# Last gate projection in 128-channel columns, mixed with row pairs by seven of the out-projection's left half

## The chip, the core and the metric

The kernel runs on one core of a Trainium2 chip, as one program. The metric is the device time of one execution in microseconds (us), as a median of several runs. The engines are called here as in the profile: PE (TensorE, matmuls), DVE (VectorE), ACT (ScalarE), POOL (GpSimd) and SP (SyncE, which here issues most transfers).

## What is computed

A decoder trunk of two layers on one sequence of 256 positions with 2048 channels, everything in float32:

```python
# each of 2 layers; x is 256 x 2048
h  = rmsnorm(x) * g
P  = h @ W_in                 # 2048 -> [q | k | v | gate_B | gate_C | conv_in], 1024 each
A  = differential attention (8 heads, q/k norm, shared relative bias)
Cv = gate_B * causal_depthwise_conv3(gate_C * conv_in)
x  = x + concat([A, Cv]) @ W_out        # 2048 -> 2048, "out-projection"
x  = x + (relu(rmsnorm(x) @ W_up) ** 2) @ W_down      # 8192 wide
```

The changed place is the projection for gate_B (the "last gate", since it is computed last of the six) and the out-projection that follows it.

## The kernel before

**Precision.** A float32 operand is split in two float32r parts, high and low, so that a = hi + lo. A product is made of three matmuls, the list `TERMS`: hi x hi, hi x lo, lo x hi. So each weight tile that arrives ("raw") costs one ACT copy, which makes the high part (L322), and one DVE subtraction, which makes the low part (L323). High and low parts rotate through three buffers each, raw tiles through four.

**Weights.** A class `Weights` holds a list of jobs in the order in which PE will want the tiles; each job issues a load on SP's queue and the two split instructions, some tiles ahead of their use. `take()` hands the next tile to the matmuls. Work that is not on PE's line (attention, norms, biases) is written as generators, and `work.tick()` between matmuls lets them emit their next instructions. So the order of instructions on each engine is fixed when the program is built, and each engine works its list in order.

**The mixer of a layer.** q, k and v come by halves, attention runs as background work, then gate_C and conv_in by quarters of 256 channels, with the convolution after each (`cv`), and then the last gate in four quarters (`linear_t`, L433, PE tile `gb`). `joined` (L445, L448) adds the two halves of the accumulator, `gate` (L742 to L745) multiplies by `cv`, and `in_parts` (L738, L739) writes the high and low parts into `cat`, the left operand of the out-projection: `cat` 0 and 1 hold attention, 2 and 3 the gated convolution.

**The out-projection** (`BySeven.project`) runs over two halves of 1024 output columns, left (g = 0) and right (g = 1), each of two chunks of 512 columns. Its 2048 input rows are eight "row pairs" of 2 x 128. An ordinary pair takes 24 matmuls of 128x512 for both chunks (L851). A pair "by seven" is taken as a product of 2x2 blocks with seven block products in place of eight (after Winograd's form of Strassen's method): 21 matmuls (L876). For that it needs sums of blocks on both sides. Left side: `sums_of` (L780 to L786), four small additions and a split. Weights: two raw tiles are loaded (L807); `w7b` is the split left tile (L793, L794), `w7t` four sums of weight blocks (L822, L823, L826, L827), `w7x` and `w7y` their splits, and half of the right tile goes through an ordinary high and low buffer (as `whi`, `wlo`). In each half two of eight pairs go by seven, those of gate quarters 0 and 1. The seven products are put together once, after the last pair by seven (`es`, `e2`, `es4`), and added to the residual `xs`. After the left half the norm of the MLP starts on the residual's first chunks (transposes `tpn`).

**The MLP's up-projection** already runs by 128-channel columns: `up_part` (L1172) uses a weight tile of 16 x 128 x 128 in two halves, and its accumulator is one PSUM bank with the tag `av`, of which there is one buffer.

Of the kernel before, what the change touches and what calls it, by code (L numbers as in the profile page):

```python
# [15 lines left out]
P = 128  # L16
# [22 lines left out]
GATED = (0, 1)  # L39
# [83 lines left out]
def trunk(ctx: ExitStack, tc: tile.TileContext, x, w_in, w_out, conv_w, q_norm_g, k_norm_g,  # L123
# [142 lines left out]
    def load_bias(l, bpool, bias, setup):  # L266
# [11 lines left out]
        for h in range(0, NH, 2):  # L278
            for j in range(2):
                late(nc.scalar.activation(bias[:, j * NH + h:j * NH + h + 2],  # L280
                                          revs[j][:, h:h + 2, ::-1], AF.Copy))
            yield 2
# [24 lines left out]
    class Weights:  # L307
# [80 lines left out]

        def turned(self, w, col):
            for i in range(D // P // 4):  # L390
                self.plain(w, 4 * P * i, col, 4)

# [217 lines left out]
    def attention(l, qT, kT, kL, v, h0, dst, bias, tmp, pace):  # L610
# [9 lines left out]
        def unit(i):  # L620
# [19 lines left out]
            for t in range(NT):  # L640
                W = (t + 1) * P
                for m in range(2):
                    nc.vector.tensor_tensor_reduce(
                        out=s[:, m, OFF[t]:OFF[t] + W], in0=sc[t][:, m],
                        in1=bias[:, 2 * h + m, S - W:], op0=ALU.add, op1=ALU.max, scale=1.0,
                        scalar=-3.0e38, accum_out=mx[:, t, m:m + 1])
# [59 lines left out]
            yield 12 * pace  # L706
            for t in range(NT):
# [4 lines left out]
                tp3 = tp.rearrange("p (h c) -> p h c", c=P)  # L712
# [22 lines left out]
    def in_parts(dst, j, value):  # L735

        hi, lo = (dst.open()[:, i, 2 * j:2 * j + 2] for i in range(2))
        nc.scalar.activation(hi, value, AF.Copy)  # L738
        nc.vector.tensor_sub(lo, value, hi.bitcast(F32))  # L739
        dst.ready = j == 1  # L740
# [10 lines left out]
    class BySeven:  # L751
# [3 lines left out]
        def __init__(self, l, bpool, weights):  # L755
            self.l, self.pool, self.weights = l, bpool, weights
            n = D // (4 * P)
            seven = [n + q for q in GATED]
            plain = [i for i in range(2 * n) if i not in seven]


            self.orders = []
            for g in range(2):
                chunks = (2 * g, 2 * g + 1)
                order = [(n, i) for n in chunks for i in plain[:2]]
                for i, j in zip(plain[2:], seven):
                    order += [("seven", j), ("pair", i)][::-1 if g else 1]
                order += [("pair", i) for i in plain[2 + len(seven):-2]]
                order += [(n, i) for n in chunks for i in plain[-2:]]
                self.orders.append(order)  # L770
            self.sums = []

        def sums_of(self, q, y):

            if len(self.sums) % 2 == 0:
                room = self.pool.tile([P, 2, 2, 4, P], F32R, tag="b", name="sf")
                self.sums += [room[:, 0], room[:, 1]]
            a11, a21, a12, a22 = (y[:, k, t * P:(t + 1) * P] for k in range(2) for t in range(NT))
            v = wide(f"sv{q}").rearrange("p (s c) -> p s c", c=P)
# [4 lines left out]
            hi, lo = (self.sums[GATED.index(q)][:, part] for part in range(2))  # L784
# [3 lines left out]
        def jobs(self, w, i, col):  # L788
# [8 lines left out]
            def two(pool, tag, name, src):  # L797

                room = pool.tile([P, 2, 2, CH], F32R, tag=tag, name=name)
# [3 lines left out]
            def plain():  # L803
# [9 lines left out]
                b11, b21 = two(self.pool, "b", "w7b", raws[0])  # L813
# [4 lines left out]
            def sums():  # L818
                left, right = mine["raw"]
                t = mine["t"] = self.pool.tile([P, 4, CH], F32, tag="b", name="w7t")  # L820
# [3 lines left out]
                made = two(apool, "a", "w7x", t[:, 0:2])  # L824
# [5 lines left out]
            def more():  # L830
                return two(apool, "a", "w7y", mine["t"][:, 2:4])
# [3 lines left out]
        def project(self, g, cat, norm, kpool, tmp):  # L835
            weights, order = self.weights, self.orders[g]
            both = [mm.tile([P, NT, CH], F32, tag="mm2", name=f"o{self.l}{2 * g + n}")
                    for n in range(2)]
            accs = [[acc[:, t] for t in range(NT)] for acc in both]
            prods = {2: accs[0][0], 4: accs[0][1], 3: accs[1][0]}  # L840

            def plain(i, n):
                hi, lo = weights.take()
                for j in range(2):
                    k = 2 * i + j
                    a = cat[k // KG]
                    while not a.ready:
                        work.tick()
                    for t in range(NT):
                        for m, (pa, pw) in enumerate(TERMS):  # L850
                            nc.tensor.matmul(  # L851
                                accs[n][t], a.ap[:, pa, k % KG, t * P:(t + 1) * P],
                                (hi, lo)[pw][:, j], start=(k == 0 and m == 0),
                                stop=(i == last and j == 1 and m == 2))
                    work.tick()

            def form(i, pa, a):
                q = i - D // (4 * P)
                if a >= S1:
                    return self.sums[GATED.index(q)][:, pa, a - S1]  # L860
                k, t = 2 * i + a // 2, a % 2
                return cat[k // KG].ap[:, pa, k % KG, t * P:(t + 1) * P]

            def seven(i, start, end):
                if start:
                    for n in (1, 5, 6):
                        prods[n] = bank(f"po{self.l}{g}{n}")
                    prods[7] = ps.tile([P, CH], F32, tag="av", name=f"po{self.l}{g}7", bufs=1)
# [3 lines left out]
                for n, a, b in ((1, A11, b11), (2, A12, b21), (3, S4, b22), (5, S1, t1),  # L872
                                (7, S3, t3), (6, S2, t2), (4, A22, t4)):
                    own = n in (1, 5, 6, 7)
                    for m, (pa, pw) in enumerate(TERMS):
                        nc.tensor.matmul(prods[n], form(i, pa, a), b[pw],  # L876
                                         start=(start and own and m == 0),
                                         stop=(end and own and m == 2))
# [4 lines left out]
            def onto(n):  # L883
                for t in range(NT):
                    nc.vector.tensor_add(xs[2 * g + n][:, t], accs[n][t], xs[2 * g + n][:, t])

            last = order[-1][1]
            steps = [i for what, i in order if what == "seven"]
            done = [j for j, (what, i) in enumerate(order) if what == 2 * g][-1]
            for j, (what, i) in enumerate(order):  # L890
                if what == "pair":
                    plain(i, 0)
                    plain(i, 1)
                elif what == "seven":
                    seven(i, i == steps[0], i == steps[-1])
                    if i == steps[-1]:

                        x11, x21, x12, x22 = (xs[2 * g + n][:, t]
                                              for n in range(2) for t in range(NT))


                        room = tmp.tile([P, 2, CH], F32, tag="ao", name="es", bufs=1)
# [582 lines left out]
```

## Time and profile before

| what | value |
|---|---|
| median of 3 runs | 2122.43 us (2122.37 to 2122.54) |
| profiled execution | 2122.24 us |
| its span from first to last instruction | 2120.4 us |
| granted TensorE clock | 1.000 |
| PE busy | 2115.1 us |
| DVE busy | 1748.2 us |
| ACT busy | 1382.2 us |
| POOL busy | 159.2 us |
| mean DMA rate | 224 GB/s |
| last gate, layer 0 (from, length) | 253.34, 44.53 us |
| last gate, layer 1 | 1307.88, 44.53 us |

Rows of the profile read as follows. A group of instructions shows line, engine, operation, output tile <- input tiles, sizes, count, then busy time and the mean nanoseconds of one, then the idle time of the engine just before them and what ended it. In the timeline a row is start, length, engine and instruction, with the idle time before it in brackets. In the chain a row is start, length and a run of instructions of one engine. In the waits a row is the waiting instruction, the one that released it, the time in total, the number of times, and the longest.

### The profile page before, as it was taken

The numbers are of one execution on the slowest core, as the hardware profiler recorded it, in microseconds if no ns is written. First come the engines' busy times: TensorE is split into PE (matmuls) and PEld (weight loads), VectorE is DVE, ScalarE is ACT, GpSimd is POOL, SyncE is SP. The second block draws the span as 40 slices with busy tenths as digits, with TensorE's granted clock in tenths as the row PEclk, the third lists the DMA queues.
The fourth block names the chain that finished last, engine by engine and source line by source line (L and its number), as shares of the span: only waits on it lengthen the run. The fifth ranks groups of instructions, "written<-read, shape, count | busy, mean of one in ns | idle before, by whom it ended". The sixth has DMA issues, their size and how long they took to land.

```text
span 2120.4 us, 29268 instructions
## 1 busy us (share of the span) xinstructions
PE 2115.1 (100%) x10845; PEld 1807.6 (85%) x10845; DVE 1748.2 (82%) x2428; ACT 1382.2 (65%) x1838; POOL 159.2 (8%) x226
## 2 busy tenths in 40 slices
PE   9999999999999999999999999999999999999999
PEld 7888888888888888888888888888888888888887
DVE  6777678898888888799766776788988888888997
ACT  6776555676776776666566765557777677675664
POOL 3010100000000000011101101000000000000110
PEclk9999999999999999999999999999999999999999
DMA  8546666787777777788655565658877777777993
GB/s 279 175 154 205 193 194 191 251 257 226 230 233 233 230 236 230 248 299 293 213 169 182 162 212 179 199 169 267 258 229 235 231 232 233 231 229 261 319 309 104
DMA packets 297744, 476.02 MB, mean 224 GB/s; under 512 B 12707, under 2 KB 193781, under 8 KB 297600
## 3 DMA queue, kind: packets, MB, share of 16 engines
q1 hardware_dynamic: 269120, 406.76, 60.1%
q0 software_dynamic: 28288, 67.24, 9.9%
q8 instruction: 85, 1.39, 0.3%
q14 instruction: 59, 0.48, 0.1%
q10 hardware_dynamic: 192, 0.15, 0.0%
HBM read 440.52 MB, written 33.58 MB: 224 GB/s over the span
## 4 chain that ended last, share of the span: by engine, by line
PE 99%; ACT 1%; issue 0%; DVE 0%; DVEq 0%
PE upc L1172 31%; PE pr L1215 14%; PE dn L1296 8%; PE o L851 6%; PE ci L433 4%; PE gc L433 4%; PE gb L433 4%; PE k L408 4%; PE q L408 4%; PE v L408 4%; PE dn L1378 2%; PE dn L1215 2%; PE pr1r L1215 2%; PE pr0r L1215 1%; PE up L1172 1%; PE upw L1172 1%
## 5 line engine op out<-in xcount | busy, mean ns | idle before, releaser
L1172 PE MATMUL upc<-nT,uhi 128*128 128x512 f32 x1920 | 454.7, 389 | 0.0
L323 DVE TENSOR_TENSOR wlo<-raw,whi 128x1024 fp32r<-128x1024 f32 x258 | 311.8, 1222 | 156.9 <-ACT whi L322 85.6
L1172 PEld LDWEIGHTS upc<-nT,uhi 128*128 128x128 f32 x1920 | 360.3, 188 | 74.7
L322 ACT ACTIVATE whi<-raw 128x1024 fp32r<-128x1024 f32 x258 | 272.8, 1059 | 230.1 <-PE gb L433 28.0
L1036 DVE TENSOR_TENSOR ulo<-uraw,uhi 128x1024 fp32r<-128x1024 f32 x256 | 311.7, 1221 | 110.7 <-ACT f L1204 91.5
L1035 ACT ACTIVATE uhi<-uraw 128x1024 fp32r<-128x1024 f32 x256 | 270.6, 1057 | 157.8 <-PE upc L1172 137.5
L1172 PEld LDWEIGHTS upc<-nT,ulo 128*128 128x128 f32 x1920 | 246.2, 191 | 9.3
L1172 PE MATMUL upc<-nT,ulo 128*128 128x256 f32 x1920 | 249.1, 283 | 0.0
L1296 PE MATMUL dn<-whi,fb 128*128 128x512 f32 x496 | 156.5, 389 | 0.0
L851 PE MATMUL o<-whi,cat 128*128 128x512 f32 x384 | 122.0, 391 | 0.0
L1061 ACT ACTIVATE b2h<-draw 128x1024 fp32r<-128x1024 f32 x83 | 88.2, 1063 | 48.5 <-PE pr L1215 41.3
L322 ACT ACTIVATE whi<-uraw 128x1024 fp32r<-128x1024 f32 x62 | 65.9, 1062 | 81.8 <-PE dn L1296 66.0
L1296 PEld LDWEIGHTS dn<-whi,fb 128*128 128x128 f32 x496 | 93.1, 188 | 19.2
L1182 ACT ACTIVATE ev<-upc 128x512 f32<-128x512 f32 x120 | 72.0, 600 | 54.5 <-PE upc L1172 54.5
L1061 ACT ACTIVATE t24h<-t 128x1024 fp32r<-128x1024 f32 x83 | 88.3, 1063 | 22.8 <-PE pr L1215 15.9
L1062 DVE TENSOR_TENSOR t24l<-t,t24h 128x1024 fp32r<-128x1024 f32 x83 | 101.1, 1218 | 1.7
L1062 DVE TENSOR_TENSOR b2l<-draw,b2h 128x1024 fp32r<-128x1024 f32 x83 | 100.9, 1215 | 1.1 <-ACT b2h L1061 1.1
L1062 DVE TENSOR_TENSOR t13l<-t,t13h 128x1024 fp32r<-128x1024 f32 x83 | 101.0, 1217 | 0.7
L1075 DVE TENSOR_TENSOR t<-draw 128x1024 f32<-128x1024 f32 x83 | 101.1, 1218 | 0.3
L1061 ACT ACTIVATE t13h<-t 128x1024 fp32r<-128x1024 f32 x83 | 88.4, 1065 | 13.3 <-DVE t L1075 2.9
L1296 PE MATMUL dn<-wlo,fb 128*128 128x512 f32 x248 | 96.5, 389 | 0.0
L1215 PE MATMUL pr<-t13h,f 128*128 128x512 f32 x240 | 93.8, 391 | 0.0
(447 smaller groups left out, 4296.3 us busy)
## 6 DMA issues: line engine op xcount, KB each, us to landing
uraw<-in_w_up_dram SPq DMA_DIRECT2D x128, 1024.0 KB, 6.3
raw<-in_w_in_dram SPq DMA_DIRECT2D x191, 512.0 KB, 4.3
draw<-in_w_down_dram SPq DMA_DIRECT2D x174, 512.0 KB, 5.2
raw<-in_w_out_dram SPq DMA_DIRECT2D x64, 512.0 KB, 4.2
uraw<-in_w_down_dram SPq DMA_DIRECT2D x62, 512.0 KB, 5.7
raw<-in_w_down_dram SPq DMA_DIRECT2D x10, 1024.0 KB, 5.4
hid0p<-f POOLq DMA_DIRECT2D x19, 512.0 KB, 3.6
fb<-hid0p POOLq DMA_DIRECT2D x19, 512.0 KB, 7.5
```

Of the source, the lines that this page charges most:

```text
L322: pair = (nc.scalar.activation(hi, raw, AF.Copy), nc.vector.tensor_sub(lo, raw, hi.bitcast(F32)))
L323: nc.vector.tensor_sub(lo, raw, hi.bitcast(F32)))
L408: nc.tensor.matmul(acc[:, t], a.ap[:, pa, k % KG, t * P:(t + 1) * P], (hi, lo)[pw][:, j], start=(k == 0 and (pa, pw) == (0, 0)), stop=(k = ...
L433: nc.tensor.matmul(acc[:, f, 0] if part else acc[:, f], wt[:, k % 4, fs], a.ap[:, 0, k % KG] if part else a.ap[:, :, k % KG], start=(part ...
L851: nc.tensor.matmul(accs[n][t], a.ap[:, pa, k % KG, t * P:(t + 1) * P], (hi, lo)[pw][:, j], start=(k == 0 and m == 0), stop=(i == last and ...
L1035: pair = (nc.scalar.activation(hi, src, AF.Copy), nc.vector.tensor_sub(lo, src, hi.bitcast(F32)))
L1036: nc.vector.tensor_sub(lo, src, hi.bitcast(F32)))
L1061: keep(nc.scalar.activation(hi, src, AF.Copy))
L1062: keep(nc.vector.tensor_sub(lo, src, hi.bitcast(F32)))
L1172: nc.tensor.matmul(acc[:, 0] if part else acc, wt[part][:, k], a.ap[:, 0, k % KG] if part else a.ap[:, :, k % KG], start=(part == 0 and kh ...
L1215: nc.tensor.matmul(prods[n], f[:, pa, a], b[pw], start=(start and m == 0), stop=(stop and m == 2))
L1296: nc.tensor.matmul(prods[p], f[:, pa, 2 * k + t], b[pw][:, n], start=(p in starts and k == 0 and m == 0), stop=(stop and k == 1 and m == 2))
```

## The change

The last gate and the left half of the out-projection become one stage with an order written out by hand, `LEFT`. The gate comes in eight columns of 128 channels ("c"), each with two raw tiles of 8 x 128 rows by 128 columns (512 KB, rows of 512 bytes) and the `av` bank as accumulator, except for the first. Between them stand the row pairs by seven, cut in two: "a" is products 1, 2, 3 and 5 (12 matmuls), "b" is products 7, 6 and 4 (9 matmuls). Six of the eight row pairs of the left half go by seven (0 to 5): four of attention and two of the gated convolution. Pairs 6 and 7 are ordinary, and the entries (chunk, pair) place their halves. The right half keeps two pairs by seven (now 2 and 3, of attention), each after an ordinary pair.

To that end: attention's output is first evicted whole (`ay`), then split, and the sums for pairs 0 to 3 are made in attention's background work; the gate is evicted, added, multiplied and split column by column; the bias tile becomes two halves in a pool of two buffers, which later holds `w7x` and `w7y`; `w7t` of the left half takes `kL`'s place; and the results of the products by seven of the left half are added to the residual after the last matmul of that half, together with the ordinary accumulators.

The diff, cut to its core:

```diff
-GATED = (0, 1)
+LEFT = (("c", 0), ("c", 1), ("a", 0), ("c", 2), ("b", 0), ("c", 3), ("a", 1), ("c", 4), ("b", 1),
+        ("c", 5), ("a", 2), ("c", 6), ("b", 2), ("c", 7), ("a", 3), ("b", 3), (0, 6),
+        ("a", 4), ("b", 4), (1, 6), (0, 7), ("a", 5), ("b", 5), (1, 7))
+SEVEN_LEFT = tuple(i for what, i in LEFT if what == "a")
+SEVEN_RIGHT = (2, 3)
...
+        def column(self, w, col):
+            def half(kh):
+                def make():
+                    raw = self.pool.tile([P, 8, P], F32, tag="raw", name="raw", bufs=RAW)
+                    nc.sync.dma_start(
+                        raw, w[kh * 8 * P:(kh + 1) * 8 * P, col:col + P].rearrange(
+                            "(k p) c -> p k c", p=P))
+                    return self.halves(raw)
...
+    def column_part(acc, acts, weights):
+        tiles = [weights.take() for _ in range(2)]
+        for part in range(2):
+            for kh, wt in enumerate(tiles):
+                for k in range(8):
+                    a = acts[kh * 2 + k // KG]
+                    nc.tensor.matmul(
+                        acc[:, 0] if part else acc, wt[part][:, k],
+                        a.ap[:, 0, k % KG] if part else a.ap[:, :, k % KG],
...
-                hi = parts[:, 0, :, t * P:(t + 1) * P]
-                nc.scalar.activation(hi, tp3, AF.Copy, scale=s_gain[:, l:l + 1])
-                nc.vector.scalar_tensor_tensor(
-                    parts[:, 1, :, t * P:(t + 1) * P], tp3, s_gain[:, l:l + 1], hi.bitcast(F32),
-                    op0=ALU.mult, op1=ALU.subtract)
+                y = wide(f"ay{h0}_{t}")
+                nc.scalar.activation(y, tp, AF.Copy, scale=s_gain[:, l:l + 1])
+                ys.append(y.rearrange("p (h c) -> p h c", c=P))
+                hi = parts[:, 0, :, t * P:(t + 1) * P]
+                nc.scalar.activation(hi, ys[t], AF.Copy)
+                nc.vector.tensor_sub(parts[:, 1, :, t * P:(t + 1) * P], ys[t], hi.bitcast(F32))
+                yield 2
+            for j in range(2):
+                sums_of(h0 // 2 + j, *(ys[t][:, 2 * j + k] for k in range(2) for t in range(NT)))
                 yield 2
...
-    def gate(q, acc, cv, dst, y):
-        g = joined(acc, f"gb{q}")
-        nc.vector.tensor_mul(y, g, cv[:, q * 2:q * 2 + 2])
-        in_parts(dst, q % 2, y)
+    def gate(c, acc, cv, dst, y):
+        ev = nat.tile([P, 2, S], F32, tag="wide", name=f"gb{c}")
+        nc.scalar.activation(ev, acc, AF.Copy)
+        nc.vector.tensor_add(y, ev[:, 0], ev[:, 1])
+        nc.vector.tensor_mul(y, y, cv[:, c])
+        hi, lo = (dst.open()[:, i, c % KG] for i in range(2))
+        nc.scalar.activation(hi, y, AF.Copy)
+        nc.vector.tensor_sub(lo, y, hi.bitcast(F32))
...
+        def left_jobs(self, w_gate, col, w):
+            for what, i in LEFT:
+                if what == "c":
+                    weights.jobs += weights.column(w_gate, col + i * P)
+                elif what == "a":
+                    made[i] = self.jobs(w, i, 0)
+                    weights.jobs += made[i][:2]
+                elif what == "b":
+                    weights.jobs += made[i][2:]
+                else:
+                    weights.plain(w, 2 * P * i, what * CH, 2)
...
+            for j, (what, i) in enumerate(LEFT):
+                if what == "c":
+                    column(i)
+                elif what == "a":
+                    b11, b21, b22 = weights.take()
+                    self.t1, self.t3 = weights.take()
+                    self.product(1, i, A11, b11, start, end)
+                    self.product(2, i, A12, b21, start, not {"a", 0} & rest)
+                    self.product(3, i, S4, b22, start, not {"a", 1} & rest)
+                    self.product(5, i, S1, self.t1, start, end)
+                elif what == "b":
+                    t2, t4 = weights.take()
+                    self.product(7, i, S3, self.t3, start, end)
+                    self.product(6, i, S2, t2, start, end)
+                    self.product(4, i, A22, t4, start, not {"b", 0} & rest)
+                    if end:
+                        add = self.results(0)
+                else:
+                    self.pair(i, [(what, accs[what])], ...)
+                    if j == len(LEFT) - 1:
+                        add()
+                        for n in range(2):
+                            for t in range(NT):
+                                nc.vector.tensor_add(xs[n][:, t], accs[n][t], xs[n][:, t])
...
-            biasp = scope.enter_context(tc.tile_pool(name="biasp", bufs=1))
+            biasp = scope.enter_context(tc.tile_pool(name="biasp", bufs=2))
...
-            for q in range(AW // WC):
-                acc = linear_t(f"gb{l}{q}", hT, weights)
-                gate(q, acc, cv, cat[2 + q // 2], ys[:, q])
-                if q in GATED:
-                    by_seven.sums_of(q, ys[:, q])
+            by_seven.left(hT, cv)
```

More of the change, by code (lines that the diff above doesn't have):

```diff
@@ L749, in trunk, with __init__ @@
     A11, A21, A12, A22, S1, S2, S3, S4 = range(8)
     class BySeven:
-        def __init__(self, l, bpool, weights):
+        def __init__(self, l, bpool, biasp, tmp, weights):
             self.l, self.pool, self.weights = l, bpool, weights
[L757 to L779, printed above, removed]
+            self.biasp, self.tmp = biasp, tmp
+            self.pairs = range(D // (2 * P))
+            plain = [i for i in self.pairs if i not in SEVEN_RIGHT]
@@ L830, in more, with form, product, pair @@
             def more():
-                return two(apool, "a", "w7y", mine["t"][:, 2:4])
+                room = self.biasp.tile([P, 2, 2, CH], F32R, tag="bias", name="w7y")
+                return two(room, mine["t"][:, 2:4])
             return [plain, sums, more]
[L835 to L843, printed above, removed]
+        def form(self, i, pa, a):
+            if a >= S1:
+                return self.sums[i][pa][:, a - S1]
+            k, t = 2 * i + a // 2, a % 2
+            return self.cat[k // KG].ap[:, pa, k % KG, t * P:(t + 1) * P]
+        def product(self, n, i, a, b, start, stop):
+            for m, (pa, pw) in enumerate(TERMS):
+                nc.tensor.matmul(self.prods[n], self.form(i, pa, a), b[pw],
+                                 start=(start and m == 0), stop=(stop and m == 2))
+        def pair(self, i, chunks, starts=(), last=False):
+            for n, accs in chunks:
+                hi, lo = self.weights.take()
                 for j in range(2):
                     k = 2 * i + j
-                    a = cat[k // KG]
+                    a = self.cat[k // KG]
                     while not a.ready:
@@ L874, in seven @@
                     own = n in (1, 5, 6, 7)
[L875 to L878, printed above, removed]
+                    self.product(n, i, a, b, start and own, end and own)
                     if n == 5:
```

218 lines of the change are left out of this document (140 added, 78 removed).

## The prediction

> **What bounds the kernel now.** The page comes first: its busy shares and its chain.
>
> ```profile
> PE 2115.1 (100%) x10845; PEld 1807.6 (85%) x10845; DVE 1748.2 (82%) x2428; ACT 1382.2 (65%) x1838; POOL 159.2 (8%) x226
> ...
> PE 99%; ACT 1%; issue 0%; DVE 0%; DVEq 0%
> ```
>
> Then the waits of PE, which say what it ever stood still for:
>
> ```profile
> PE warm L177 <- DVE mhalf L169: 1.1, 1, 1.1
> PE q L408 <- ACT whi L348: 0.2, 1, 0.2
> ```
>
> PE multiplies from end to end and waits 1.3 us, all at the start. So a removed matmul is worth its whole spacing, and every stall that the new order makes costs its whole length. The windows of the stage that changes in layer 0 (last gate, first and second part of the out-projection) and, last, of the MLP's up-projection show how much room the feeding engines have:
>
> ```profile
> 253.30:297.90 44.60, 44.60 (x258) 39.44 (x257) 30.72 (x42) 22.84 (x27) 2.15 (x1) 1.00 0.59 189
> 297.90:347.00 49.10, 49.10 (x220) 40.63 (x220) 39.31 (x46) 25.50 (x33) 0.00 (x0) 1.00 0.62 195
> 347.00:397.00 50.00, 50.00 (x252) 42.13 (x251) 43.93 (x65) 31.05 (x48) 0.89 (x2) 1.00 0.62 206
> 408.00:480.00 72.00, 72.00 (x388) 62.46 (x387) 68.14 (x93) 51.56 (x63) 3.22 (x5) 1.00 0.78 246
> ```
>
> After the length come the busy times of PE, PEld, DVE, ACT and POOL. DVE has 14 of 44.6 us free beside the gate and 10 of 49 beside the left half. The up-projection, which already mixes 128-channel columns with products by seven, has 68.14 of 72 on DVE and still no PE wait. The granted clock is 1.00 throughout, so the clock is no part of this.
>
> **What is saved.** The chain in order of time gives the matmul spacings:
>
> ```profile
> 253.34 44.53 PE gb L433 x256
> ...
> 373.22 10.88 PE o L851 x48
> ...
> 424.33 5.54 PE upc L1172 x32
> ```
>
> A 128x512 matmul follows the last one after 10.88/48 = 0.2267 us. An ordinary row pair over both chunks takes 24 of them, by seven 21. The left half goes from two pairs by seven to six: 4 x 3 = 12 fewer in each layer, 24 in all, 24 x 0.2267 = 5.44 us. The gate keeps its 256 matmuls a layer; 32 of the old form take 44.53/8 = 5.566, 32 of the column form (the up-projection's) 5.54: 16 columns save 0.42. Saved on PE: **5.86 us**, 0.28% of the time. Nothing else on PE changes its count.
>
> **What is added off PE.** Rows for the prices:
>
> ```profile
> L323 DVE TENSOR_TENSOR wlo<-raw,whi 128x1024 fp32r<-128x1024 f32 x39 | 46.9, 1221 | 21.4 <-issue 14.6 <-ACT whi L322 5.9 <-PE gb L433 0.9
> L322 ACT ACTIVATE whi<-raw 128x1024 fp32r<-128x1024 f32 x37 | 39.2, 1060 | 36.0 <-PE gb L433 14.1 <-PE o L851 13.8 <-issue 5.4
> L794 DVE TENSOR_TENSOR w7y<-w7t,w7y 128x1024 fp32r<-128x1024 f32 x4 | 4.9, 1224 | 0.1
> L793 ACT ACTIVATE w7b<-raw 128x1024 fp32r<-128x1024 f32 x4 | 4.2, 1060 | 8.4 <-DMA raw<-in_w_out_dram 8.4
> L822 DVE TENSOR_TENSOR w7t<-raw 128x512 f32<-128x512 f32 x4 | 2.7, 686 | 0.3 <-DMA raw<-in_w_out_dram 0.3
> L786 DVE TENSOR_TENSOR sf<-sv,sf 128x512 fp32r<-128x512 f32 x2 | 1.4, 686 | 0.0
> L1183 DVE TENSOR_TENSOR h<-ev 128x256 f32<-128x256 f32 x128 | 53.1, 417 | 0.0
> L445 ACT ACTIVATE gb0l<-gb 128x512 f32<-128x512 f32 x2 | 1.2, 600 | 1.6 <-PE gb L433 1.6
> ```
>
> So DVE takes 1.22 for 1024 elements, 0.68 for 512, 0.42 for 256; ACT 1.06 for 1024 and 0.60 for an eviction. One pair by seven is three DVE subtractions of 1.22 and five of 0.68: 7.1 us, against 21 x 0.2267 = 4.76 on PE: DVE loses 2.3 on each. A column costs DVE 2 x 1.22 + 3 x 0.42 = 3.7 against 5.54. Over the left stage (174 x 0.2267 + 8 x 5.54 = 83.8 us of PE) that is 6 x 7.1 + 8 x 3.7 + four ordinary splits 4.9 + sums for two pairs 3.6 = 81 us at full durations. Consecutive instructions overlap, as ACT's timeline shows (1.06 long, the next begins 0.98 later), and by 0.08 on each of some 120 the sum falls to about 72. DVE is therefore 86 to 97% full: the average just fits. What decides is order, as DVE and ACT work their lists in order. The timeline of ACT beside the old gate:
>
> ```profile
> 260.83 1.06 ACT L322 ACTIVATE whi<-raw 128x1024 fp32r<-128x1024 f32 x1 [2.69 <-PE gb L433]
> 262.64 1.06 ACT L322 ACTIVATE whi<-raw 128x1024 fp32r<-128x1024 f32 x1 [0.75 <-PE gb L433]
> 264.51 0.60 ACT L445 ACTIVATE gb0l<-gb 128x512 f32<-128x512 f32 x1 [0.81 <-PE gb L433]
> 266.35 1.06 ACT L322 ACTIVATE whi<-raw 128x1024 fp32r<-128x1024 f32 x1 [1.24 <-PE gb L433]
> 267.33 0.63 ACT L738 ACTIVATE cat<-ys 128x512 fp32r<-128x512 f32 x1
> ```
>
> ACT stands 2.69 us at a weight split until PE leaves a buffer (three high and three low parts rotate), and whatever is listed behind stands too. Below, c0 to c7 are the columns, a0 to a5 and b0 to b5 the two parts of a pair by seven (12 and 9 matmuls).
>
> **Step 1: a2 waits for its weights, 2.7 us a layer.** In the built order ACT has, behind the eviction of c4: w7x of a2, the split of c6's first half, w7y of a2, the sums' high part, a cat part, and only then w7b of a2; DVE has w7y, c6's first half, the sums, cat, w7b. Yet PE needs w7b first, right after c5. The split of c6's first half needs the buffer that c5's first half leaves: 8 x 0.2267 = 1.81 after c5's start. From there: w7y's high part starts 0.98 later and ends at 3.85; then on DVE w7y 1.22, c6 1.22, sums 0.68, cat 0.42, w7b 1.22 = 4.76, less 4 x 0.08. End 8.3, with the handovers between engines 8.3 to 8.7. PE comes to the product with w7b's low part at 5.54 + 0.23 = 5.77. Late by 2.5 to 2.9; I take 2.7. Nothing hides it: PE has nothing else, since its own list is in order as well.
>
> **Step 2: evictions behind loads, 1.9 us a layer.** Columns c1 to c7 share one PSUM bank, so c2 starts only after the eviction of c1. That stands on ACT behind both splits of c2 and w7y of a0. The raw buffers (four) are the chain:
>
> ```profile
>   ACT w7b L793: 17.8, 8
> ...
> DMA to landing us min/median/max: 3.3/4.3/10.3
> ```
>
> ```profile
> raw<-in_w_in_dram SPq DMA_DIRECT2D x19, 512.0 KB, 3.6
> ```
>
> (first the view of the raw tile: ACT waited 17.8 us in 8 cases for a raw load; then one row of the DMA view of 230 to 400 us, the gate's loads, median 3.6). The low split of c0's second half ends at the earliest 0.3 after c0's start (its buffer leaves PE before the last low pass, 8 x (5.54 - 16 x 0.2267)/16 = 0.96 ahead of it; then 1.22). Then: load for a0 4.3, two w7t 1.29, an addition of 128x512 0.6, low split of c1's second half 1.22 (it stands on DVE behind w7t), load for c2 4.6, its high split 1.06, w7y 0.98, eviction 0.60 = 14.65; end 14.95. PE could start c2 at 2 x 5.54 + 2.72 = 13.80. Late by 1.15, with handovers some 1.4. Behind that eviction on ACT are queued c3's splits and the cat parts, so they come later by as much. With loads at the fast end of 3.3 it is nothing; with column loads a microsecond slower 2.6. The same figure returns at c4, where c3's eviction stands behind c4's splits, w7y of a1, a cat and the sums: reckoned on from the late c2, 0.5 (0 to 2.7). A load of a column's half has 512-byte rows; before has none of such size, and its rows of 1 KB and more have the median 4.3, which is why I take 4.6 here.
>
> The Trainium skill, page "DMA: Bandwidth & Descriptors", sections "Specifications" and "Why small descriptors are slow (HBM only)", says that 512 B is the least for line rate on the one hand, and that each packet costs some 3 cycles on top of its 32-byte beats on the other: 19 cycles for 512 B against 35 for 1 KB, by my estimate 9% more for the same bytes. By the first a column's load would cost what others do and c2 would come 0.3 earlier; by the second it would be 4.7. No run so far shows such a load.
>
> **Step 3: tail and seam, 0.9 us a layer.** At the stage's end ten raw tiles are wanted in some 25 us through four buffers: 10 x 4.3/4 = 11 fits, but each behind another's split: 0.4 (0 to 1.5). The results of products by seven now all come after b5: ten DVE steps of 0.60 to 0.68, behind two splits of 1.22, before the residual's first chunk is whole. From the sixth product (0.6 before b5's end) that is 8.4 to 9.2, thus 7.8 to 8.6 after b5, while PE works off (1,7) and two pairs of the right half, 36 x 0.2267 = 8.16, and then transposes that chunk: 0.5 (0 to 1.0).
>
> Edits at nothing: sums for pairs 0 to 3 inside attention, whole attention output first (a few 0.68s on DVE, whose stage has room and no PE wait); biases in two buffers; the same bytes on SP's queue, POOL's multiplications unmoved.
>
> **Sum.** 2.7 + 1.9 + 0.9 = 5.5 a layer, 11.0 for two; layer 1 has the same lists but for one exchange. 2122.24 (the profiled execution: span 2120.4 and 1.8 around it) - 5.86 + 11.0 = 2127.4; the median stands 0.2 above that execution: **2127.6 us**. Ends: only step 1, 2122.4 - 5.86 + 5.4 = 2122.0; everything at its upper end, (2.9 + 5.3 + 2.5) x 2 = 21.4, 2138. A measurement of this kernel tells about 0.2%, 4.2 us, from no change: faster is below 2118.2, slower above 2126.7.
>
> **Rivals.**
> Faster: no stall, as in the up-projection, which has the same interleaving at 95% of DVE and no PE wait. What speaks against it: there one load feeds two columns, so half as many loads stand ahead of evictions, and step 1's order is not found there. 2122.4 - 5.86 = 2116.6; it decides if w7b's low part is done by 5.8 us after c5's start. Up to 1.6 us of stalls would still be faster (2118.2). 0.15.
> No change that can be told: step 1, and of the others 0 to 2 us a layer: 2122 to 2126; half of step 1 alone would give 2119.3. Speaks for it that the gate's loads land in 3.6. 0.33.
> Slower, as forecast or worse: 0.52. The worse half is slow 512-byte rows: each column load a microsecond longer lengthens steps 2 and 3 by about 2 us a layer: 2131.5, and up to 2138. Speaks for it the maximum of 10.3; against it the low DMA share of 0.6.
> That fewer matmuls are saved is excluded by the built order: 174 for 186 in each layer.
>
> **The numbers.** The range from 2118 leaves out nearly all of the faster rival (0.14), up to 2136 some 0.06. The forecast's own range is 2126.7 to 2136.
>
> **What would show it.** PE's waits, 1.3 us now, should hold a2's product on DVE's w7b with two times 2.5 to 2.9; columns c2 and c4 on ACT's eviction; the transposes on DVE's residual add. PE's busy time should fall by 5.9. Wrong am I if the waits stay under 6 us in sum, most of all if w7b shows none; then DVE's or ACT's order was not the limit. If column loads take over 5.5, the time goes to the upper end.

## Result and the profile after

The changed kernel takes **2141.44 us** (median of 4 runs, 2139.46 to 2142.54) against 2122.40 before (4 runs, 2122.29 to 2122.54): ratio 1.0088, 95% interval 1.0074 to 1.0103, 19.0 us slower. The forecast was 2127.6 with a range up to 2136. The sign was right, the size was not: the loss against the saving of 5.86 us is 24.9, and 11.0 had been forecast.

Busy time and chain on the page of the changed kernel:

```profile
PE 2119.0 (99%) x10821; PEld 1805.0 (84%) x10821; DVE 1794.7 (84%) x2540; ACT 1405.0 (66%) x1886; POOL 171.3 (8%) x226
...
PE 89%; DVE 5%; DMA 4%; issue 1%; ACT 1%; SPq 0%; DVEq 0%; ACTq 0%
```

The count of matmuls fell by 24, as forecast (10845 to 10821), but PE's busy time rose by 3.9 us where it should have fallen by 5.9: on average a matmul stands longer. And a tenth of the chain, which was nearly all PE, now lies elsewhere (the chain follows a late result back through work that ran beside PE, so this share is not idle time). The waits of PE:

```profile
PE po L887 <- DVE w7b L833: 4.4, 2, 2.2
PE gb L417 <- ACT gb L774: 3.6, 4, 1.3
PE po L887 <- ACT w7b L832: 2.7, 2, 1.8
PE po L901 <- DVE wlo L327: 2.2, 3, 1.1
PE tpn L511 <- DVE x L1005: 1.7, 2, 1.2
...
PE po L887 <- DVE w7y L833: 0.9, 1, 0.9
PE o L901 <- DVE wlo L327: 0.8, 2, 0.5
```

Sixteen waits, 16.3 us (before: 1.3, at the start, and those are still there). Three of these rows are the three steps of the prediction by name: w7b for a2, the evictions of columns (`gb`) for c2 and c4, and the residual (`x`) for the transposes. Now the same stage by windows (start:end, length, PE, PEld, DVE, ACT, POOL busy, granted clock, DMA share, GB/s); the second and the last row are the stretch in which a2 is late, in layer 0 and in layer 1:

```profile
253.60:299.20 45.60, 43.65 (x235) 37.16 (x234) 38.90 (x63) 25.79 (x35) 7.09 (x1) 1.00 0.64 189
299.20:307.60 8.40, 4.44 (x14) 3.36 (x14) 6.73 (x9) 3.56 (x6) 0.00 (x0) 0.80 0.55 166
307.60:354.96 47.36, 44.59 (x208) 36.31 (x207) 37.12 (x48) 23.61 (x29) 0.00 (x0) 1.00 0.49 162
1319.00:1365.00 46.00, 44.34 (x242) 37.94 (x240) 40.40 (x63) 26.73 (x38) 7.10 (x1) 1.00 0.64 192
1365.00:1375.50 10.50, 7.33 (x19) 5.54 (x19) 7.51 (x11) 4.82 (x7) 0.00 (x0) 0.67 0.50 155
```

Elsewhere in these stages the granted clock is 1.00. In single microseconds of that stretch it is 0.50:

```profile
304.00:305.00 1.00, 1.00 (x3) 0.81 (x3) 1.00 (x2) 0.00 (x0) 0.00 (x0) 0.50 0.85 262
```

And PE's own timeline there, in layer 0:

```profile
297.13 2.07 PE L417 MATMUL gb<-nT,wlo 128*128 128x256 f32 x16
300.97 0.50 PE L887 MATMUL po<-w7b,cat 128*128 128x512 f32 x1 [1.77 <-ACT w7b L832]
303.66 2.50 PE L887 MATMUL po<-w7b,cat 128*128 128x512 f32 x5 [2.19 <-DVE w7b L833]
305.96 0.63 PE L887 MATMUL po<-whi,sf 128*128 128x512 f32 x1
```

Five matmuls from 303.66 to 305.96 are 0.46 apart (0.2267 in the forecast); those at half clock in layer 1 are 0.43 apart. So three costs stand on each other:

- idle time, 16.3 us in 16 places;
- a restart at each: from the start of the last matmul before a wait to the first behind it lie some 0.16 us more than spacing and named wait (a matmul's length in the timeline, 0.39, less its spacing), and the first matmuls behind take 0.11 to 0.15 longer than their spacing (268.94 to 272.72 for a column's 16, 3.78 against 3.65 undisturbed). 16 x 0.27 = 4.3 us;
- the half clock behind a2: matmuls at nearly twice their spacing, 1.3 us more in layer 0 and 2.9 in layer 1, 4.2 in all.

16.3 + 4.3 + 4.2 - 5.9 = 18.9. The profiled execution's span grew by 20.4 (2120.4 to 2140.8); 0.4 of that is a later start of the first layer, some 1 us stays open (delays too short for the waits view may be part of it).

### The profile page after: what moved, and what is told of

It is laid out like the page before. It is cut to its first block, busy times and chain, and to the rows that moved or that the text cites. A ratio compares the mean times of both kernels' runs of the same rounds, so it can differ in the third digit from the quotient of the medians.

```text
span 2140.8 us, 29393 instructions
## 1 busy us (share of the span) xinstructions
PE 2119.0 (99%) x10821; PEld 1805.0 (84%) x10821; DVE 1794.7 (84%) x2540; ACT 1405.0 (66%) x1886; POOL 171.3 (8%) x226
## 4 chain that ended last, share of the span: by engine, by line
PE 89%; DVE 5%; DMA 4%; issue 1%; ACT 1%; SPq 0%; DVEq 0%; ACTq 0%
PE upc L1299 31%; PE pr L1342 13%; PE dn L1423 8%; PE gc L465 4%; PE k L440 4%; PE ci L465 4%; PE q L440 4%; PE v L440 4%; DMA raw<-in_w_out_dram 3%; PE dn L1505 2%; PE dn L1342 2%; PE o L901 2%; DVE wlo L327 2%; PE pr1r L1342 2%; PE pr0r L1342 1%
## 5 line engine op out<-in xcount | busy, mean ns | idle before, releaser
L327 DVE TENSOR_TENSOR wlo<-raw,whi 128x1024 fp32r<-128x1024 f32 x242 | 293.4, 1222 | 111.0 <-ACT whi L326 75.7
L326 ACT ACTIVATE whi<-raw 128x1024 fp32r<-128x1024 f32 x242 | 255.5, 1059 | 195.1 <-PE v L440 22.1
L327 DVE TENSOR_TENSOR wlo<-uraw,whi 128x1024 fp32r<-128x1024 f32 x62 | 75.8, 1223 | 17.9 <-ACT whi L326 17.6
```

Of the source, the lines that this page charges most:

```text
L326: pair = (nc.scalar.activation(hi, raw, AF.Copy), nc.vector.tensor_sub(lo, raw, hi.bitcast(F32)))
L327: nc.vector.tensor_sub(lo, raw, hi.bitcast(F32)))
```

## Experiments

All times are medians, and ratios are against runs of the kernel before on the same chip (2122.40 to 2122.76). For comparison: the changed kernel 2141.44.

**1. Is a2 late by order?** The pool `b` has eight buffers, for the four cat tiles, `cv`, two tiles of sums and w7b, so none to spare; in the built order w7b of a2 stands directly behind the first write to the fourth cat tile.

```diff
+                if c == 3:
+                    nc.gpsimd.memset(self.cat[3].open()[:, 0, 0, 0:1].bitcast(F32), 0.0)
```

> The split of a2's left weights (w7b) stands behind the first write to the fourth cat tile in both lists, as if the weight tile got its buffer only after that one. Here a one-element POOL memset opens that cat tile two columns earlier; the built order then has w7b of a2 right after c5's first split. Theory (order, not load and not throughput): both waits of PE on a2's w7b (3.96 us in layer 0, 3.16 in layer 1) go, with them four restarts of 0.27 and the stretch at half clock behind each (1.7 and 3.0 us), together 12.9: 2141.4 - 12.9 = 2128.5, clock 1.000 everywhere. Rival (a2's left tile lands too late, or DVE is simply too full): PE waits 2.5 us or more at a2 again, or the same time turns up as waits behind it; time 2137 or more.

2130.15 us (2129.23 to 2133.11), ratio 1.0038 (1.0023 to 1.0053): 11.3 us less for one element written early. DVE and PE at a2 in layer 0:

```profile
289.92 1.23 DVE L833 TENSOR_TENSOR w7b<-raw,w7b 128x1024 fp32r<-128x1024 f32 x1 [1.32 <-ACT w7b L832]
```

```profile
298.78 1.55 PE L887 MATMUL po<-w7b,cat 128*128 128x512 f32 x6
```

w7b's low part is done at 291.1, 7.6 us before a2, where it had come 4.4 us after PE wanted it (303.6 against 299.2); no wait on w7b is left in either layer, and the clock around a2 is 1.00. So the order, not the load and not DVE's load, made a2 late. The rival is right in one point: new waits appear on w7y of pairs 3 and 4, and in layer 1 two of them close together bring half clock again:

```profile
1382.00:1386.00 4.00, 1.87 (x7) 1.05 (x6) 3.94 (x5) 2.25 (x3) 0.00 (x0) 1.00 0.81 253
1386.00:1390.00 4.00, 4.00 (x12) 3.14 (x11) 3.86 (x6) 2.11 (x2) 0.00 (x0) 0.57 0.56 158
```

**2. Is it idle time that halves the clock?** Sixteen matmuls by a tile of zeros stand ahead of a2 in each layer (the edit cut to its core):

```diff
+                    if i == 2:
+                        for _ in range(16):
+                            nc.tensor.matmul(self.prods[1][0:64], self.zeros, self.cat[0].ap[:, 0, 0:2],
+                                             start=False, stop=False)
                     self.product(1, i, A11, b11, start, end)
```

> The changed kernel with 16 matmuls of 512 columns by a zero operand (they add zero to the first product) ahead of a2 in each layer, 16 x 0.2267 = 3.6 us of PE work put where PE stood idle. Nothing else is moved. Theory (the idle of about 5 us in 5 makes PE run at half clock for 3 to 6 us afterwards): PE is busy until the low part of w7b comes, a2 begins no earlier, but the matmuls behind it run at 0.2267 and the clock shows 1.00: 1.7 + 3.0 less, plus two restarts of 0.27 less: 2141.4 - 5.2 = 2136.2. Rival (the half clock has another cause, such as the load of DVE or a free-running cycle): clock 0.5 behind a2 as before and a time of 2141 or more.

2132.09 us (2130.58 to 2133.98), ratio 1.0045 (1.0030 to 1.0060). The windows over the same stretch of layer 0:

```profile
298.80:307.20 8.40, 8.40 (x39) 6.14 (x39) 7.19 (x10) 3.87 (x6) 0.00 (x0) 1.00 0.56 172
```

39 matmuls in 8.4 us where the changed kernel did 14, and clock 1.00 for 0.80: PE kept busy with zeros is not slowed. That much is shown. The gain of 9.4 us is more than the 5.2 expected, and it is not all clock: with the longer PE list the planner, which fixes the order on each engine when the program is built, also placed instructions behind a2 in another order on ACT and DVE, and the waits on w7y and on the splits of ordinary halves (2.8 us in layer 0) and on the residual (1.7) are absent. So this kernel shows that the clock follows the idle time, but not the clock's price by itself.

**3. Evictions first.** `tc.issue_after(x)` puts what is issued under it behind x on x's engine, here behind the eviction of the column before:

```diff
+                    if kh and c in (2, 4):
+                        with tc.issue_after(evicted[0].ins):
+                            return self.halves(raw)
```

and the same for w7y of pairs 0 and 1.

> On ACT the evictions of columns 1 and 3 are put ahead of the second split of the following column and of w7y (order only, nothing is taken away). Theory of step 2: the waits of PE at c2 and c4 on the eviction (1.34 and 0.61 us in layer 0, 1.03 and 0.63 in layer 1) go, with four restarts of 0.27: 4.7 us less, 2136.7, if what was late next is not late too. Rival: the column's second half or w7y, which now come later by an eviction, or the load behind them, take over the wait; then under 2 us are gained. a2's wait may grow by what c2 and c4 lose, since DVE gets less time: with that the time stays within 1 us of 2141.4.

2138.32 us (2135.68 to 2141.12), ratio 1.0078 (1.0061 to 1.0095). The waits on evictions fall from 3.6 to 0.2 us, so step 2's place was right; the time falls by about 3, with a wide spread, since a2 stays late (4.2 and 2.8 us on w7b) and half clock lasts 6.83 us in layer 0 and 3.41 in layer 1.

**4. The seam.** 

> At the end of the left half the four additions to the residual's chunk 0 come before those to chunk 1 (the same twelve additions in another order). Theory of the seam: the first transposes of chunk 0 wait 1.24 and 0.46 us for DVE now; two DVE additions of 0.6 fewer stand ahead of them, so the waits fall to about 0 and two restarts go: 2.2 us less, 2139.2, and less than the spread of the runs can show by time alone; the trace decides. Rival: the splits of the right half's tiles, not the additions, hold the chunk; waits as before.

2141.26 us (2139.62 to 2142.71). The planner built the same order on every engine from the edited text, so this tested nothing of the seam. It is a second measurement of the changed kernel, and tells one thing: in its profile the clock is at 0.50 from 301.44 to 308.26 in layer 0 (changed kernel: 303.08 to 306.49) after less idle time on w7b than there (2.9 against 4.0 us). So the same program loses more or less to the clock from run to run.

The traces of all runs together say what this hangs on. The clock falls to 0.50 eleven times in mid-kernel. Each stretch lasts 3.41 or 6.83 us, and where one trace has two, their starts lie a whole multiple of 3.413 us apart (changed kernel: 303.08 and 1368.04, 312 times). So the clock changes on a grid of 3.41 us. Laid on that grid, the windows read like this (the third value from the end is the clock; length less PE's busy time is idle time; the last two rows are layer 1 of experiment 10):

```profile
299.67:303.08 3.41, 0.50 (x1) 0.19 (x1) 3.41 (x5) 2.67 (x4) 0.00 (x0) 1.00 0.09 21
303.08:306.49 3.41, 2.83 (x7) 2.27 (x8) 2.85 (x5) 0.42 (x1) 0.00 (x0) 0.50 0.91 262
306.49:309.91 3.42, 3.42 (x17) 2.81 (x16) 0.01 (x1) 1.10 (x2) 0.00 (x0) 1.00 0.50 186
...
1375.96:1379.37 3.41, 1.52 (x7) 0.94 (x5) 2.62 (x6) 0.96 (x2) 0.00 (x0) 1.00 0.39 148
1379.37:1382.78 3.41, 2.14 (x8) 1.60 (x9) 3.41 (x5) 3.41 (x5) 0.00 (x0) 1.00 0.10 19
```

Ahead of each of the eleven stretches PE was idle for 1.7 us or more of one such window. No mid-kernel window with less brought half clock (the most is 1.64 us), and a single one with more did not: the 1.90 us shown here, where a wait of 2.44 us lies across a border of the grid. Half clock goes on for a second window when the first has 0.67 us of idle time or more (five cases) and ends after one at 0.58 or less (six). So where a wait falls on the grid decides too, and that differs from run to run.

The runs of this program lie 3 us apart. Part of such a spread goes with the clock (in experiment 1 the run of 2129.23 us has a mean granted clock of 1.000, the run of 2133.11 one of 0.998), but not all: the runs of experiments 6 and 8 lie 3.6 and 2.7 us apart at 1.000.

**5 to 7. Both orders, and the tail.** With the edits of 1 and 3 together:

> Both orders together: cat tile opened early (a2's weights in time) and the evictions of columns 1 and 3 first. If the two steps are separate terms of the sum, the waits on the eviction that remained with the first edit alone (2.5 us in three places, and 0.27 for each restart) go as well: 2130.2 - 3.3 = 2126.9; the waits of PE on w7y of the fourth and fifth row pair (4.4 us) stay, and with them any half clock they bring. Rival (the average load of DVE decides, the place only moves the wait): what goes at c2 and c4 comes back on w7y or on the tail's splits; 2129 or more.

2129.61 us (2127.39 to 2131.04, 7 runs), ratio 1.0032 (1.0021 to 1.0043). The rival was nearer: the waits on evictions went from 2.5 to 1.3 us, but those on w7y from 4.4 to 4.9. Then b4 moved behind an ordinary half, which is one entry of `LEFT`:

```diff
-        ("a", 4), ("b", 4), (1, 6), (0, 7), ("a", 5), ("b", 5), (1, 7))
+        ("a", 4), (1, 6), ("b", 4), (0, 7), ("a", 5), ("b", 5), (1, 7))
```

> As the former, and b4 is moved behind the ordinary half (1,6), so that four and a half more row products lie between a4 and b4 (2.7 us of PE work without seven's sums). Theory (order): w7y of that pair is in time, the waits of 2.6 us there go with their restarts and the half clock that followed them in layer 1: 2126.9 - 4 to 5 = 2122 to 2123, no change against the kernel before, or a little faster. Rival (DVE is full in this stage, 86 to 97%): the wait moves to a5 or b5; 2126 or more.

2123.79 us (2122.05 to 2125.67, 10 runs), ratio 1.0005 (0.9996 to 1.0014): no change against the kernel before. All that is left of PE's waits in it, apart from the start:

```profile
PE po L895 <- DVE w7y L838: 2.1, 3, 0.8
...
PE gb L420 <- ACT gb L779: 0.6, 1, 0.6
```

Clock 1.00 throughout. Compared with the changed kernel 17.7 us came back without a matmul, a load or a byte less: three edits of order. That it is no faster than the kernel before has its reason in the trace: in the gate and the out-projection the starts of its matmuls still lie 5.3 us further behind their spacing than there, which uses up most of the 5.86 saved. The waits listed are 2.7 us of that, their restarts about 1.1, and the rest is delays of less than 0.3 us each.

Five pairs by seven in place of six, with pair 5's first ordinary half right behind a3, went the other way (the edit against the kernel just shown):

```diff
-        ("c", 7), ("a", 3), ("b", 3), (0, 6),
-        ("a", 4), (1, 6), ("b", 4), (0, 7), ("a", 5), ("b", 5), (1, 7))
+        ("c", 7), ("a", 3), (0, 5), ("b", 3), (0, 6),
+        ("a", 4), (1, 5), ("b", 4), (1, 6), (0, 7), (1, 7))
```

> As the first of this set, but five row pairs by seven in place of six: pair 5 is ordinary, its halves lie between a3 and b3 and between a4 and b4. 3 matmuls of 0.2267 more in each layer (1.36 us for both), 2.3 us less work that DVE cannot hide. Theory (order and tail): no waits behind c7, clock 1.00: 2122.6 - 5.86 + 1.36 = 2118.1, plus at most 2 us of rests: 2118 to 2120, faster than the kernel before. Rival (idle comes from the columns, or from loads): 2124 or more.

2130.86 us (2128.88 to 2133.97), ratio 1.0038 (1.0024 to 1.0052). The time is the rival's: DVE has less to do, but the low split of (0, 5) comes late, and PE waits for it once in each layer, long enough for the half clock. In layer 0 its high part is done at 312.8, but on DVE it stands behind w7b of pair 4, whose tile landed only at 315.8. So place and load make this wait together:

```profile
PE po L909 <- DVE wlo L327: 5.8, 2, 3.3
```

**8. Columns alone.** `LEFT` with two pairs by seven, as before the change (its entries written short, c0 for ("c", 0)):

```diff
+LEFT = (c0, c1, a0, c2, b0, c3, (0, 2), c4, a1, c5, b1, c6, (0, 3), c7, (1, 2), (1, 3),
+        (0, 4), (1, 4), (0, 5), (1, 5), (0, 6), (1, 6), (0, 7), (1, 7))
```

> The changed kernel with the columns but only two row pairs by seven in the left half, as before (0 and 1; a0 and b0 stay where they are, pair 1 comes between c4 and c6, ordinary halves of pairs 2 and 3 between other columns). None of the order edits. Saved on PE: only the 0.42 of the columns. Theory: columns cost nothing themselves; the wait at c2 on the eviction behind a0's loads stays (1.3 and 1.0 us and two restarts), the one on w7b is gone, since pair 2 is ordinary: 2122.0 + 2.8 = 2124.8, clock 1.00. Rival (128-channel columns with one bank and 512-byte loads stall by themselves): waits on evictions at most columns, 2130 or more.

2126.02 us (2124.69 to 2127.36, 10 runs), ratio 1.0017 (1.0007 to 1.0026). Its waits beyond the start:

```profile
PE gb L417 <- ACT gb L774: 2.1, 3, 1.1
```

As expected within 1.2 us: columns themselves run, and most of what PE waits for is c2's bank, that is the eviction which stands on ACT behind a0's loads (0.81 and 1.10 us). So the rest of the 19 us comes from mixing six pairs by seven into them.

**9 to 12. Is there a better version?** Five pairs with the ordinary halves behind b3; the tail's splits pinned in the order of use; evictions of c2 and c4 ahead of a1's and a2's right weight tile, for six and for five pairs. `late` keeps an instruction where the program writes it. The three edits (the second also covers the ordinary halves of the left part):

```diff
-        ("a", 3), (0, 5), ("b", 3), (0, 6), ("a", 4), (1, 5), ("b", 4), ...
+        ("a", 3), ("b", 3), (0, 5), (0, 6), ("a", 4), (1, 5), ("b", 4), ...
```

```diff
-                nc.scalar.activation(hi, src, AF.Copy)
-                nc.vector.tensor_sub(lo, src, hi.bitcast(F32))
+                pair = (nc.scalar.activation(hi, src, AF.Copy),
+                        nc.vector.tensor_sub(lo, src, hi.bitcast(F32)))
+                if not col and i >= 3:
+                    for ins in pair:
+                        late(ins)
```

```diff
+                if not col and i in (1, 2):
+                    with tc.issue_after(evicted[0].ins):
+                        return b11, b21, split(hi[:, 0], lo[:, 0], raws[1][:, 1])
```

> Five pairs by seven with both order edits, but the halves of pair 5 stand behind b3 as two ordinary halves with (0,6) (entries (0,5), (0,6) after b3; (1,5) between a4 and b4), so that no ordinary split is wanted right behind a3, where the former five-pair order waited 3.3 and 2.5 us. Theory (what the stage costs is the places at which a split comes late, not the columns and not the number of pairs): no wait of 1 us or more, clock 1.00, 2122.6 - 5.86 + 1.36 = 2118.1 plus rests of 2 us: 2118 to 2120.5, faster than the kernel before by about 0.1%. Rival (raw tiles through four buffers come too slowly for three ordinary halves in a row): a wait of 2 us on the split of (0,6), 2123 or more.

> As the kernel with b4 behind an ordinary half, and in addition the splits of pairs 3 to 5 and of the ordinary halves of the left part are kept on ACT and DVE in the order in which PE wants them. Theory: the remaining waits on w7y (0.5 us in layer 0, 1.6 in layer 1) are order and go, 2123.8 - 3 = 2121; with 24 matmuls fewer and all rests gone it could not come below 2116.7. Rival (strict order makes DVE stand behind loads): waits on w7b or on the splits of 1 us and more, 2125 or more.

> Six pairs by seven, both order edits and b4 behind an ordinary half, and the evictions of columns 2 and 4 are put ahead of the split of the right weight tile of a1 and a2, whose load they stand behind in the two kernels before this. Theory: the waits at c3 and c5 go (0.6 us in layer 0 here), the rests on w7y (2.1 us) stay: 2123.8 - 1 = 2122.8; no change against the kernel before. Rival (these waits are what keeps DVE's tail in time): w7y grows by as much, 2123.8.

> The same for the five-pair order with its halves behind b3. Theory: the waits on evictions there (2.4 us in three places, with 0.27 each for the restart) go: 2124.7 - 3.2 = 2121.5, the waits of 1.0 and 0.7 us on the split of (0,6) stay; faster than the kernel before by 1 us, under what can be told. Rival (the wait moves to the split of (0,6), since the raw tiles come no sooner): 2124 or more.

| kernel | us | ratio (95%) | PE's main waits in its profile |
|---|---|---|---|
| five, halves behind b3 | 2124.71 | 1.0011 (1.0002 to 1.0021) | evictions 2.4, split 1.7 |
| six, tail pinned | 2132.17 | 1.0048 (1.0031 to 1.0065) | split of (0,6): 4.6 on its high part |
| six, evictions 2 and 4 | 2125.61 | 1.0013 (1.0004 to 1.0021) | w7y 2.2, evictions 1.1 |
| five, evictions 2 and 4 | 2125.59 | 1.0015 (1.0006 to 1.0024) | split 2.5, eviction 0.5 |

All four forecasts missed to the slow side, by 3 to 11 us. The rival came true in place and time for the pinned tail and for five pairs with the evictions ahead, in time alone for the first row (its wait on (0, 6) is 1.0 us, not 2), and not for the third, whose waits on w7y stayed at 2.2. A wait went where an edit had pushed it from, and another came up, as on an ordinary split (4.6 and 2.5 us in the second and the fourth row). Strict order of use was the worst of them. ACT's timeline in layer 0 of the pinned kernel:

```profile
313.92 0.58 ACT L779 ACTIVATE gb<-gb 128x512 f32<-128x512 f32 x1
319.09 0.42 ACT L783 ACTIVATE cat<-y 128x256 fp32r<-128x256 f32 x1 [4.59 <-DVE y L781]
319.41 1.04 ACT L326 ACTIVATE whi<-raw 128x1024 fp32r<-128x1024 f32 x1
```

ACT stood 4.59 us at a column's part of cat, for DVE's product, and the split of (0, 6), pinned behind it, began only at 319.41. On DVE that product stood in turn behind weight sums of the next pair that waited for a load:

```profile
317.43 0.69 DVE L870 TENSOR_TENSOR w7t<-raw 128x512 f32<-128x512 f32 x1 [1.36 <-DMA raw<-in_w_out_dram]
318.04 0.69 DVE L871 TENSOR_TENSOR w7t<-raw 128x512 f32<-128x512 f32 x1
318.64 0.42 DVE L781 TENSOR_TENSOR y<-y,cv 128x256 f32<-128x256 f32 x1
```

No version beat the kernel before; the best is its equal.

## Why the prediction was wrong in size

- **The saving** was right: 24 matmuls fewer in the counts, and away from waits and half clock their spacing is still 0.227 us.
- **Step 1** named the right place, engine and cause (w7b behind w7y, sums and cat), and sized it too small: 2.7 us forecast, 3.96 and 3.16 measured. The failing piece is the clause "w7y's high part starts 0.98 later". It assumed that w7y's input was ready. ACT shows it was not:

```profile
295.56 1.07 ACT L326 ACTIVATE whi<-raw 128x1024 fp32r<-128x1024 f32 x1 [1.50 <-PE gb L417]
298.09 1.06 ACT L832 ACTIVATE w7y<-w7t 128x1024 fp32r<-128x1024 f32 x1 [1.46 <-DVE w7t L868]
```

The split of c6 began 2.06 us after c5's start (293.50), near the forecast (1.81); w7y began 4.59 after it, not 2.79, since the fourth weight sum on DVE came late. The chain of waits goes on from there to DVE's first weight sum at 291.6, which had stood 2.4 us for a load of 6.39 us (285.19 to 291.58). The forecast left the raw loads out of this step and in step 2 only.
- **Step 2** was right in place and nearly in size: c2 1.34 and 1.03 us (1.4 forecast), c4 0.61 and 0.63 (0.5). The chain is the one written down: load of a0's right tile landed 259.5, two sums, the addition, c1's low split done 262.6, load (262.61 to 266.29), c2's second split 266.40, w7y, eviction from 268.31, c2 at 268.94.
- **Step 3**: the seam 1.24 and 0.46 (0.5 forecast); the tail 3.1 us in layer 0 and 0.8 in layer 1 (0.4 forecast). Two loads of the chain fall into it that took 6.73 and 5.80 us (from 314.82 and from 329.06). The column loads took 4.4 us in the median (3.6 to 5.8), near the 4.6 taken. The loads of 2-KB rows in this stage, for which 4.3 was taken, rose further: to a median of 5.6 in layer 0 and 5.0 in layer 1, against 4.2 and 4.1 in the same stage before. Whether that is a cause of the late tail or goes with its order, no run separates; with b4 moved (experiment 6) they took 4.6 in layer 0. So the rows show no price of the 512-byte rows, and they do not decide between the two sections of the Trainium skill that were quoted.
- **The sum of idle times** was 11.0 forecast, 16.3 measured. For both layers the terms are: step 1 7.1 (5.4 forecast), step 2 3.6 (3.8), the seam 1.7 (1.0), the tail 3.9 (0.8). So the term most mis-sized is the tail.
- **What was missing altogether is 8.5 of the 13.8 us by which the forecast was too low**: the restarts (4.3) and the half clock (4.2). Two steps failed here. One is that every stall "costs its whole length": it cost some 0.27 us more, 16 times. The other is the sentence "The granted clock is 1.00 throughout, so the clock is no part of this." In the stages looked at, the trace of before could show no other value, as PE never stood in them; it was read as a constant, though the forecast itself put 2.5 to 2.9 us of idle time in one place. A sign stands at the end of the trace of before, where the clock falls to 0.50 at 2118.70, 2.1 us after the end of the last matmul:

```profile
2116.50:2118.70 2.20, 0.07 (x1) 0.00 (x0) 0.87 (x2) 0.00 (x0) 0.00 (x0) 1.00 0.29 103
2118.70:2120.44 1.74, 0.00 (x0) 0.00 (x0) 0.00 (x0) 0.00 (x0) 0.00 (x0) 0.50 0.06 20
```

The Trainium skill, page "TensorE: Matmul & The Clock Gate", section "Part 1: The HAM clock gate (the "warmup" mystery)", says that the clock is gated to one half after an idle window of about 3.4 us and freed after as long a busy one. By that rule a wait of 2.7 alone would have been free of it. The traces agree in the two values (0.50 and 1.00) and in the length of a window (3.41 us). They differ in how much idle it takes: 1.7 us within a window were enough (experiment 5, layer 1), and so was one wait of 2.5 us in layer 1 of experiment 7.
- **The rivals.** The fast side fell: that the up-projection runs without a stall told nothing of this stage, whose order on DVE and ACT is another. That slow column loads decide did not come true (4.4 us); how much of the tail hangs on the longer loads of 2-KB rows stays open. That the price of one wait is more than its length was on neither list.

Open: a measurement of the half clock's price by itself (the 4.2 us are counted from spacings, and experiment 2 moved other instructions as well), and the part of the tail that hangs on loads.

## To carry to other kernels

Where one engine runs without a gap, a new wait on it costs its length and about 0.27 us for a restart. Where such waits put some 1.7 us of idle time or more into one window of 3.41 us, as they did here, expect a stretch at half clock of one or two windows behind them. Put all three into the sum, and multiply by the number of places. In a stage like this one, with a helper engine 86 to 97% full, the place of each instruction in the engines' lists decides, not the average; read the built order for each tile that PE wants next, and look for what made it stand there, which may be a buffer of a quite different tile. Follow such a chain back to the last load, every time.

## Not expected of the hardware

- Half clock after 1.7 to 2.9 us of idle time within one window of 3.41 us, lasting one or two such windows (3.41 or 6.83 us), in a kernel that otherwise runs at 1.00; filling the gap with 16 matmuls by zero kept it at 1.00.
- Any stall costs more than the waits view names: some 0.16 us ahead of and 0.11 to 0.15 us behind a wait.
- Runs of the kernels with stalls spread over 2.7 to 5.4 us, those of the kernel before over 0.25 to 1.4.
